# Last product of a SwiGLU layer by pairs of column blocks, part of it with seven products for eight; gate2 multiply-adds moved; SiLU as one activation

## The chip, the cores and the metric

The kernel runs on one core of a Trainium2 chip. The metric is the device time of one execution in microseconds, the median of several runs. Before the change it is 1625.05 us (three runs, 1624.05 to 1626.1).

## What is computed

One layer of a decoder trunk for 256 tokens of width 2048, in float32. The change touches its last part, the feed-forward network, and the vector gate2 that scales its result:

```python
gate, up = jnp.split(h @ w_ffn_in, 2, axis=-1)      # (256, 2048) @ (2048, 2 * 5632)
y = (jax.nn.silu(gate) * up) @ w_ffn_out            # (256, 5632) @ (5632, 2048)
x = x + gate2 * y                                   # gate2: 2048 numbers of silu(c) @ w_ada
```

Everything ahead of it (norms, three token mixers, their projections) is the same in both kernels.

## The kernel before

**Matmuls in three pieces.** Each float32 operand is kept as a rounded half `hi` and a remainder `lo`; `mm3` (L169 to L172) makes a product of three matmuls, hi x hi (L170), hi x lo (L171), lo x hi (L172). The activations stand in the array, transposed, 128 x 128 at a time; the weights move through it in 512 columns. A "chunk" is 128 of the inner dimension, a "column block" 512 output columns, and the 256 tokens are two tiles.

**Weights.** A DMA on SP's queue (`raw_tile`, L159) brings two chunks of one column block, 512 KB. The scalar engine rounds them to `whi` (L166), the vector engine subtracts to get `wlo` (L167; a "split" in the text). `whi` and `wlo` have four buffers each (`halves_room`), `raw` has four too, and in the FFN's first product two scratch tiles, A4 and A8, serve as further raw tiles. A split's buffers come free when TensorE is through with the weights four splits back. In `block` one such pair of chunks serves twelve matmuls: two chunks, two token tiles, three pieces.

**FFN, first product.** Eleven rounds `i` (L1283 on): in each a column block of gate (`pg`) and one of up (`pu`), sixteen chunks each, into four PSUM banks `acc`. In the rounds 1 to 10 the first four chunks of both blocks go through `chain`: the two token tiles and the two column blocks make a 2 x 2 product over two pairs of chunks, and it is done in Winograd's form of Strassen's scheme with seven products instead of eight. Seven splits are needed for it and four differences of weights (`right_sums`, L1220), and for the left side four sums, made once (`left_sums`). Partial results are added between banks (L1246, the copies L1261 and L1264); one bank, c21, gathers and is handed over several times, so a product into it waits for the addition before. The chain's first matmuls follow the round before without a pause; `later` (called behind the fifth product) transposes the activations of the round before (L1071) and splits them (L190, L191) into H, A, T and other slots. After the chain come `block(pg ...)` and `block(pu ...)` over twelve chunks. The gate block's PSUM goes through Sigmoid (L1292) and a multiply (L1293), the up block's through another multiply (L1305).

**gate2.** A generator in the background computes it (32 multiply-adds of 1024 columns on the vector engine, L287, then additions of the bias, L936, and a broadcast over the partitions with two matmuls for each half of a quarter, L945 to L952). `tick` moves it on: 0.4 of a step for each call. `block` calls it every two chunks, `chain` after each product. `flush` runs what is left, behind the first column block of the last product.

**Last product.** Four column blocks `n`, 44 chunks each, one after the other through `block`, two PSUM banks each; then `add_out` multiplies with gate2 (L1329), adds the residual (L1331) and stores. n = 3 runs its last chunks token tile by token tile, so that the end is short.

**What sets the order.** A scheduler orders each engine's queue at build time by priority: inside `prio()` instructions are put ahead as if they had been written some 4000 instructions earlier (weight loads, casts, splits, evictions), as far as their buffers allow. Every queue then runs strictly in that order.

## Time and profile before

| | |
|---|---|
| median of three runs | 1625.05 us |
| the profiled execution's own time | 1625.11 us |
| its span on the core | 1623.3 us |
| mean granted clock of TensorE | 0.995 |
| TensorE busy | 1597.2 us, 7293 matmuls |
| vector engine busy | 1215.9 us |
| scalar engine busy | 839.9 us |
| FFN's first product, rounds 1 to 10 | from about 936 to 1379 us |
| last product | from about 1379 us to the end |

All times in timelines are microseconds from the span's start. A row of a timeline has the start, the length, the engine, the line, the operation with output and inputs (buffer numbers left out), and in brackets how long the engine had idled before it and what ended that. A matmul's length is more than its share of the engine: matmuls are pipelined, and what one costs is the distance to the next one's start. The vector and scalar engines likewise start an instruction a little before the one ahead has ended. In a row of groups "x18 | 12.1, 684" means 18 instructions, 12.1 us busy, 684 ns each.

### The profile page before, as it was taken

To read this page: it belongs to the slowest core of one execution; us is meant where nothing else is said; L and a number is where in the kernel's file an instruction comes from. 1 tells how busy PE (TensorE), PEld (TensorE's weight loads), DVE (VectorE), ACT (ScalarE), POOL (GpSimd) and SP (SyncE) were. 2 spreads that over 40 slices of the span, in tenths; PEclk is the share of its full clock that TensorE was granted. 3 is DMA by queue.
4 is the path that set the end of the run, shared out by engine and by line. 5 is a ranking of instruction groups with operands and counts; after the bars stand their busy time and mean duration, and the time that the engine had idled before them with its cause. 6 is when DMAs were issued, how large, how long until landed. Compare 5 with 4: busy or idle time off the path is not lost.

```text
span 1623.3 us, 20048 instructions
## 1 busy us (share of the span) xinstructions
PE 1597.2 (98%) x7293; PEld 1316.6 (81%) x7293; DVE 1215.9 (75%) x1396; ACT 839.9 (52%) x1162; POOL 5.3 (0%) x14
## 2 busy tenths in 40 slices
PE   8999999999999999999999999999999999999999
PEld 7878888788777888888887888777888888888887
DVE  6889995887779787878757788988877776454454
ACT  5654458756587444444445555545555555333332
POOL 1000000000000000000000000000000000000000
PEclk9999999999999999999999999999999999999999
DMA  8999996884777888988777578777666667666663
GB/s 333 351 328 320 329 308 222 279 261 141 248 235 233 263 306 309 316 291 309 241 220 228 172 248 274 256 263 244 191 187 192 196 195 234 192 204 194 205 207 113
DMA packets 116179, 399.24 MB, mean 246 GB/s; under 512 B 13090, under 2 KB 13896, under 8 KB 116080
## 3 DMA queue, kind: packets, MB, share of 16 engines
q1 hardware_dynamic: 115856, 397.95, 74.6%
q8 instruction: 57, 0.93, 0.2%
q14 instruction: 42, 0.34, 0.1%
q0 software_dynamic: 224, 0.01, 0.0%
HBM read 393.71 MB, written 4.19 MB: 245 GB/s over the span
## 4 chain that ended last, share of the span: by engine, by line
PE 87%; DVE 5%; DMA 3%; ACT 2%; issue 2%; SPq 0%; DVEq 0%; ACTq 0%
PE acc L172 27%; PE acc L171 27%; PE acc L170 27%; DVE ada L287 2%; DVE wlo L167 1%; DMA AR<-ada_rest 1%; DMA raw<-w_ffn_in 1%; PE misc L1071 1%; ACT whi L166 1%; PE misc L786 1%; DMA A<-ada 1%; PE misc L171 0%; PE misc L170 0%; PE misc L172 0%; DMA raw<-w_in 0%
## 5 line engine op out<-in xcount | busy, mean ns | idle before, releaser
L167 DVE TENSOR_TENSOR wlo<-raw,whi 128x1024 fp32r<-128x1024 f32 (+1 forms) x486 | 577.3, 1195 | 295.7 <-ACT whi L166 294.1
L166 ACT CAST whi<-raw 128x1024 fp32r<-128x1024 f32 (+1 forms) x486 | 499.3, 1030 | 563.8 <-PE acc L172 443.1
L171 PE MATMUL acc<-wlo,H 128*128 128x512 f32 x1476 | 578.8, 392 | 2.5 <-DVE wlo L167 2.3
L172 PE MATMUL acc<-whi,H 128*128 128x512 f32 x1476 | 579.2, 393 | 1.0 <-DVE H L1157 0.6
L170 PE MATMUL acc<-whi,H 128*128 128x512 f32 x1476 | 578.2, 392 | 0.8 <-ACT H L442 0.4
L171 PEld LDWEIGHTS acc<-wlo,H 128*128 128x128 f32 x1476 | 278.4, 189 | 61.0 <-DVE wlo L167 4.4
L172 PEld LDWEIGHTS acc<-whi,H 128*128 128x128 f32 x1476 | 278.5, 189 | 59.6 <-DVE H L449 1.8
L170 PEld LDWEIGHTS acc<-whi,H 128*128 128x128 f32 x1476 | 278.5, 189 | 58.6 <-ACT H L442 1.3
L170 PE MATMUL acc<-whi,A 128*128 128x512 f32 x372 | 147.2, 396 | 4.5 <-DVE acc L1246 4.5
L171 PE MATMUL acc<-wlo,A 128*128 128x512 f32 x372 | 145.5, 391 | 0.6 <-DVE wlo L167 0.6
L166 ACT CAST whi<-A 128x1024 fp32r<-128x1024 f32 x90 | 94.5, 1054 | 89.1 <-PE acc L172 76.2
L167 DVE TENSOR_TENSOR wlo<-A,whi 128x1024 fp32r<-128x1024 f32 x90 | 109.1, 1222 | 33.5 <-ACT whi L166 32.8
L172 PE MATMUL acc<-whi,A 128*128 128x512 f32 x340 | 133.0, 391 | 0.0
L170 PEld LDWEIGHTS acc<-whi,A 128*128 128x128 f32 x372 | 70.1, 188 | 19.8 <-DVE acc L1246 6.0
L171 PEld LDWEIGHTS acc<-wlo,A 128*128 128x128 f32 x372 | 70.2, 189 | 15.2 <-DVE wlo L167 1.4
L287 DVE SCALAR_TENSOR_TENSOR ada<-AR,csil,ada 128x1024 f32<-128x1024 f32 x59 | 75.3, 1281 | 8.0 <-DMA AR<-ada_rest 7.9
L172 PEld LDWEIGHTS acc<-whi,A 128*128 128x128 f32 x340 | 64.1, 189 | 13.6
L170 PE MATMUL acc<-whi,T 128*128 128x512 f32 x120 | 46.7, 389 | 0.0
L171 PE MATMUL acc<-wlo,T 128*128 128x512 f32 x120 | 46.7, 389 | 0.0
L172 PE MATMUL acc<-whi,T 128*128 128x512 f32 x120 | 46.7, 389 | 0.0
L172 PE MATMUL acc<-whi,OS 128*128 128x512 f32 x112 | 43.6, 389 | 0.0
L486 ACT COPY A<-acc 128x512 f32<-128x512 f32 x50 | 29.0, 586 | 14.3 <-PE acc L172 13.0
(369 smaller groups left out, 1412.7 us busy)
## 6 DMA issues: line engine op xcount, KB each, us to landing
raw<-w_in SPq DMA_DIRECT2D x203, 512.0 KB, 5.0
raw<-w_ffn_in SPq DMA_DIRECT2D x122, 512.0 KB, 4.7
raw<-w_ffn_out SPq DMA_DIRECT2D x88, 512.0 KB, 4.2
AR<-ada_rest SPq DMA_DIRECT2D x79, 512.0 KB, 5.0
A<-w_ffn_in SPq DMA_DIRECT2D x54, 512.0 KB, 4.7
raw<-w_out SPq DMA_DIRECT2D x32, 512.0 KB, 4.6
KC<-ada_rest SPq DMA_DIRECT2D x30, 512.0 KB, 5.6
OS<-ada SPq DMA_DIRECT2D x16, 512.0 KB, 6.7
```

The source lines that it names most:

```text
L166: nc.scalar.copy(hi, raw)
L167: state["split"] = nc.vector.tensor_tensor(lo, raw, hi.bitcast(F32), op=ALU.subtract)
L170: nc.tensor.matmul(ps, lh, rh, start=start, stop=False, skip_group_check=seeded)
L171: nc.tensor.matmul(ps, lh, rl, start=False, stop=False, skip_group_check=seeded)
L172: state["mm"] = nc.tensor.matmul(ps, ll, rh, start=False, stop=stop, skip_group_check=seeded)
L287: nc.vector.scalar_tensor_tensor(acc, raw, c, acc, op0=ALU.mult, op1=ALU.add)
L486: nc.scalar.copy(A[b][:, t, :], pss[t])
L786: nc.tensor.matmul(ps[:n, t * N_GLA + h, :].rearrange("p (s l) -> p s l", l=L), at(f, h, t)[:, :n], odd(at(f, h, t)), start=True, stop=True,)
L1071: nc.tensor.transpose(ps[:, i, :], src[:, i * P : (i + 1) * P], ident)
```

## The change

Three things are changed. Lines named after L1200 have other numbers in the changed kernel: the differences are L1226 there, the last difference in its own place is L1242, the left side's sums L1207 to L1214, the additions between banks L1252, the multiply with the up block L1315, the load of the residual L1327, Silu L1303, and `add_out` L1339 and L1341.

1. The last product goes by pairs of column blocks (0 and 1, 2 and 3). The first eight chunks of each pair (four of its 22 chunk pairs) go through `chain` with seven products, each over two groups of chunk pairs, so each product has 12 matmuls. The left side's sums for it are made in the rounds 8 and 9, of the activations of the rounds 0 and 1, in the slots KC, AR0, AR1 and A15. The scratch tiles are A13, A14, H2 and H3, and H4 to H7 serve as further raw tiles; H0 to H7 hold the FFN's input until its first product is over.
2. `chain` no longer calls `tick`.
3. Sigmoid and multiply become one activation, Silu. The differences use two scratch tiles a group instead of three in turn.

```diff
@@ -1197,13 +1197,14 @@
     state["rate"] = RATE_FFN
     ring["tags"] = ("AR0", "AR1", "KC")
     act = []
-
-    sums = [S(tag, [P, 4, 2, P], F32R) for tag in ("A2", "A3")]
-
-    def left_sums(hi, lo):
-
-        full, raw = S("A13", [P, 4, T]), S("A14", [P, 4, 2, P])
-        nc.vector.tensor_tensor(full, h2[0][0].bitcast(F32), h2[1][0].bitcast(F32), op=ALU.add)
+    act_sums = []
+    LATE = {8: ("KC", "AR0"), 9: ("AR1", "A15")}
+
+    def left_sums(tags, scratch, xh, xl):
+
+        hi, lo = (S(tag, [P, 4, 2, P], F32R) for tag in tags)
+        full, raw = S(scratch[0], [P, 4, T]), S(scratch[1], [P, 4, 2, P])
+        nc.vector.tensor_tensor(full, xh.bitcast(F32), xl.bitcast(F32), op=ALU.add)
         (a0, a1), (b0, b1) = ([full[:, c : c + 2, t * P : (t + 1) * P] for t in range(NT)] for c in (0, 2))
         nc.vector.tensor_tensor(raw[:, 0], a1, b1, op=ALU.add)
         nc.vector.tensor_tensor(raw[:, 1], raw[:, 0], a0, op=ALU.subtract)
@@ -1211,33 +1212,38 @@
         nc.vector.tensor_tensor(raw[:, 3], b0, raw[:, 1], op=ALU.subtract)
         nc.scalar.copy(hi, raw)
         nc.vector.tensor_tensor(lo, raw, hi.bitcast(F32), op=ALU.subtract)
-
-    def right_sums(src, b0, b1):
-
-        def differ(x, y):
-            d = S(f"A{13 + state['turn'] % 3}", [P, 2, NB])
-            state["turn"] += 1
-            nc.vector.tensor_tensor(d, x, y, op=ALU.subtract)
-            return d
+        return hi, lo
+
+    def right_sums(src, b0, b1, places):
 
         def halved(raw):
             hi, lo = halves_room()
             halve(hi, lo, raw)
             return hi, lo
 
+        def differ(tag, x, y):
+            d = S(tag, [P, 2, NB])
+            nc.vector.tensor_tensor(d, x, y, op=ALU.subtract)
+            return d
+
+        out = []
         with prio():
-            b11, b12 = raw_tile(src, 0, b0), raw_tile(src, 0, b1)
-            b22, b21 = raw_tile(src, 2, b1), raw_tile(src, 2, b0)
-            out = [halved(b11)]
-            t1 = differ(b12, b11)
-            out.append(halved(t1))
-            t2 = differ(b22, t1)
-            out += [halved(t2), halved(b21)]
-            out.append(halved(differ(b22, b12)))
-            out += [halved(b22), halved(differ(b21, t2))]
+            raws = [(raw_tile(src, 4 * g, b0), raw_tile(src, 4 * g, b1)) for g in range(len(places))]
+            raws = [r + (raw_tile(src, 4 * g + 2, b0), raw_tile(src, 4 * g + 2, b1)) for g, r in enumerate(raws)]
+            out += [halved(b11) for b11, b12, b21, b22 in raws]
+            t1 = [differ(p[0], r[1], r[0]) for p, r in zip(places, raws)]
+            out += [halved(t) for t in t1]
+            t2 = [differ(p[1], r[3], t) for p, r, t in zip(places, raws, t1)]
+            out += [halved(t) for t in t2]
+            out += [halved(r[2]) for r in raws]
+            out += [halved(differ(p[0], r[3], r[1])) for p, r in zip(places, raws)]
+            out += [halved(r[3]) for r in raws]
+            for t, r in zip(t2, raws):
+                nc.vector.tensor_tensor(t, r[2], t, op=ALU.subtract)
+            out += [halved(t) for t in t2]
         return out
 
-    def chain(lefts, rights, c11, c21, c12, c22):
+    def chain(lefts, sums, rights, c11, c21, c12, c22):
 
         side, held = misc_bank([P, NB]), scr([P, NB])
 
@@ -1248,14 +1254,15 @@
         rights = iter(rights)
 
         def product(ps, left, first=False):
-            hi, lo = next(rights)
-            for i in range(2):
-                h, l = left(i)
-                mm3(ps, h, l, hi[:, i, :], lo[:, i, :], first and i == 0, i == 1, seeded=True)
-            tick(state["rate"])
-
-        total = lambda q: lambda i: (sums[0][:, q, i, :], sums[1][:, q, i, :])
-        part = lambda c, t: lambda i: lefts(c + i, t)
+            for g in range(len(sums)):
+                hi, lo = next(rights)
+                for i in range(2):
+                    h, l = left(g, i)
+                    begin, end = first and g == i == 0, g == len(sums) - 1 and i == 1
+                    mm3(ps, h, l, hi[:, i, :], lo[:, i, :], begin, end, seeded=True)
+
+        total = lambda q: lambda g, i: (sums[g][0][:, q, i, :], sums[g][1][:, q, i, :])
+        part = lambda c, t: lambda g, i: lefts(4 * g + c + i, t)
         product(c11, part(0, 0), True)
         with prio(2 * AHEAD):
             nc.scalar.copy(c21, c11)
@@ -1267,12 +1274,12 @@
         product(c11, part(2, 0))
         product(c21, total(2))
         add(c22)
-        with tc.issue_after(state["mm"].ins), prio():
-            later.pop()()
+        if later:
+            with tc.issue_after(state["mm"].ins), prio():
+                later.pop()()
         product(c12, total(3))
         product(c21, part(2, 1))
 
-    state["turn"] = 0
     for i in range(NFF):
         pg = [acc_bank() for _ in range(NT)]
         if i == 0:
@@ -1283,18 +1290,21 @@
             pu = [acc_bank() for _ in range(NT)]
         else:
             pu = [acc_bank() for _ in range(NT)]
-            chain(h2_at, right_sums(w_ff, i, NFF + i), *pg, *pu)
+            chain(h2_at, h2_sums, right_sums(w_ff, i, NFF + i, [("A13", "A14")]), *pg, *pu)
+            if i in LATE:
+                assert not macs
+                with prio():
+                    act_sums.append(left_sums(LATE[i], ("A13", "A14"), *act[i - min(LATE)]))
             block(pg, h2_at, w_ff, 4, KC, i, go_on=True, seeded=True)
         sgs = []
         with prio():
             for t in range(NT):
                 sg = scr([P, NB])
-                nc.scalar.activation(sg, pg[t], AF.Sigmoid)
-                nc.vector.tensor_mul(sg, sg, pg[t])
+                nc.scalar.activation(sg, pg[t], AF.Silu)
                 sgs.append(sg)
         if i == 0:
             block(pu, h2_at, w_ff, 0, KC, NFF)
-            left_sums(*sums)
+            h2_sums = [left_sums(("A2", "A3"), ("A13", "A14"), h2[0][0], h2[1][0])]
             rooms["extra"] = ("A4", "A8")
         else:
             block(pu, h2_at, w_ff, 4, KC, NFF + i, go_on=True, seeded=True)
@@ -1335,29 +1345,35 @@
     KF = 4 * NFF
     CUT = KF - 14
     w_fo = I["w_ffn_out"]
+    K0 = 4 * len(act_sums)
     for n in range(4):
-        pss = [acc_bank() for _ in range(NT)]
+        if n % 2 == 0:
+            rooms["extra"] = ("H4", "H5", "H6", "H7")
+            both = [[acc_bank() for _ in range(NT)] for _ in range(2)]
+            rights = right_sums(w_fo, n, n + 1, [("A13", "A14"), ("H2", "H3")])
+            chain(act_at, act_sums, rights, *both[0], *both[1])
+        pss = both[n % 2]
         if n == 3:
-
-            block(pss, act_at, w_fo, 0, CUT, n, more=True)
+            rooms["extra"] = ()
+            block(pss, act_at, w_fo, K0, CUT, n, more=True, go_on=True, seeded=True)
             w = load_weights(w_fo, CUT, KF, n, spare=[f"H{j}" for j in range(2, 8)])
-            block(pss, act_at, None, CUT, KF, 0, w=w, tiles=(0,), go_on=True)
+            block(pss, act_at, None, CUT, KF, 0, w=w, tiles=(0,), go_on=True, seeded=True)
             with prio():
                 add_out(n, 0, pss[0])
 
-            block(pss, act_at, None, CUT, KF - LASTK, 0, w=w, tiles=(1,), go_on=True, more=True)
+            block(pss, act_at, None, CUT, KF - LASTK, 0, w=w, tiles=(1,), go_on=True, more=True, seeded=True)
             side = acc_bank()
             for cols, ps in ((slice(0, NB - LASTC), pss[1][:, : NB - LASTC]), (slice(NB - LASTC, NB), side[:, :LASTC])):
                 for k in range(KF - LASTK, KF):
                     wh, wl = w[k - CUT]
                     h, l = act_at(k, 1)
-                    mm3(ps, h, l, wh[:, cols], wl[:, cols], k == KF - LASTK and cols.start > 0, k == KF - 1)
+                    mm3(ps, h, l, wh[:, cols], wl[:, cols], k == KF - LASTK and cols.start > 0, k == KF - 1, seeded=True)
                 if cols.start == 0:
                     add_out(n, 1, pss[1], end=NB - LASTC)
                     add_out(n, 1, pss[1], NB - LASTC, store=False)
             add_out(n, 1, side, NB - LASTC, base=NB - LASTC)
         else:
-            block(pss, act_at, w_fo, 0, KF, n)
+            block(pss, act_at, w_fo, K0, KF, n, go_on=True, seeded=True)
             if n == 0:
                 flush()
                 gate2 = state["gate2"]
```

How the change moves instructions, at three places. On the vector engine behind the chain of round i = 9, where TensorE goes on to `block(pg ...)` and needs its first split. Before, from behind the last split of the chain (acc is the PSUM addition, wlo a split, OS2 and OS1 the transposed activations of the round before):

```order
L1246 TENSOR_TENSOR acc_2323_10920<-acc_2322_10919,scr_2348_10967 128x512
L167 TENSOR_TENSOR wlo_2343_10957<-raw_2327_10926,whi_2342_10956 128x1024
L167 TENSOR_TENSOR wlo_2346_10963<-A15_2344_10960,whi_2345_10962 128x1024
L1246 TENSOR_TENSOR acc_2324_10921<-acc_2322_10919,scr_2348_10967 128x512
L167 TENSOR_TENSOR wlo_2353_11031<-raw_2351_11028,whi_2352_11030 128x1024
L191 TENSOR_TENSOR OS2_2320_10915<-misc_2349_11002,OS1_2319_10914 128x4x128
L191 TENSOR_TENSOR OS2_2320_10915<-misc_2350_11009,OS1_2319_10914 128x4x128
L167 TENSOR_TENSOR wlo_2356_11037<-A4_2354_11034,whi_2355_11036 128x1024
```

Now (A13 and A14 are scratch, A5 and A6 activations of round 1, A15 and AR1 the new sums):

```order
L1252 TENSOR_TENSOR acc_2307_10857<-acc_2306_10856,scr_2331_10903 128x512
L167 TENSOR_TENSOR wlo_2327_10894<-raw_2312_10865,whi_2326_10893 128x1024
L167 TENSOR_TENSOR wlo_2329_10899<-A14_2318_10877,whi_2328_10898 128x1024
L1252 TENSOR_TENSOR acc_2308_10858<-acc_2306_10856,scr_2331_10903 128x512
L1207 TENSOR_TENSOR A13_2336_10966<-A5_1788_8422,A6_1789_8423 128x1024
L191 TENSOR_TENSOR OS2_2304_10852<-misc_2332_10938,OS1_2303_10851 128x4x128
L191 TENSOR_TENSOR OS2_2304_10852<-misc_2333_10945,OS1_2303_10851 128x4x128
L1209 TENSOR_TENSOR A14_2337_10967<-A13_2336_10966 128x256
L1211 TENSOR_TENSOR A14_2337_10967<-A13_2336_10966 128x256
L1210 TENSOR_TENSOR A14_2337_10967<-A14_2337_10967,A13_2336_10966 128x256
L167 TENSOR_TENSOR wlo_2340_10978<-raw_2338_10975,whi_2339_10977 128x1024
L1212 TENSOR_TENSOR A14_2337_10967<-A13_2336_10966,A14_2337_10967 128x256
```

The next block's first split stood right behind the PSUM addition; now the first of the new sums, the two splits of the transposed activations and three additions stand ahead of it.

On the vector engine at the start of the last product. Before (scr is the product of gate and up, H1 and H0 are the activations of round 10):

```order
L167 TENSOR_TENSOR wlo_2458_11511<-raw_2456_11508,whi_2457_11510 128x1024
L167 TENSOR_TENSOR wlo_2469_11603<-raw_2467_11600,whi_2468_11602 128x1024
L167 TENSOR_TENSOR wlo_2472_11609<-raw_2470_11606,whi_2471_11608 128x1024
L167 TENSOR_TENSOR wlo_2475_11615<-raw_2473_11612,whi_2474_11614 128x1024
L1305 TENSOR_TENSOR scr_2439_11472<-scr_2439_11472,acc_2393_11256 128x512
L1305 TENSOR_TENSOR scr_2440_11475<-scr_2440_11475,acc_2394_11257 128x512
L167 TENSOR_TENSOR wlo_2478_11621<-raw_2476_11618,whi_2477_11620 128x1024
L167 TENSOR_TENSOR wlo_2481_11627<-raw_2479_11624,whi_2480_11626 128x1024
L167 TENSOR_TENSOR wlo_2484_11633<-raw_2482_11630,whi_2483_11632 128x1024
```

Now (H5 and H7 hold the first column block of the first and the second group, H6 and raw_2464 the second, H2, H3, A13 and A14 differences):

```order
L946 TENSOR_TENSOR T6_2450_11498<-ada_1706_7984,T6_2450_11498 128x256
L167 TENSOR_TENSOR wlo_2470_11582<-H5_2461_11565,whi_2469_11581 128x1024
L1226 TENSOR_TENSOR A13_2473_11589<-H6_2462_11567,H5_2461_11565 128x1024
L1226 TENSOR_TENSOR A14_2479_11601<-raw_2466_11575,A13_2473_11589 128x1024
L1315 TENSOR_TENSOR scr_2430_11432<-scr_2430_11432,acc_2383_11210 128x512
L1315 TENSOR_TENSOR scr_2431_11434<-scr_2431_11434,acc_2384_11211 128x512
L1226 TENSOR_TENSOR H2_2474_11591<-raw_2464_11571,H7_2463_11569 128x1024
L167 TENSOR_TENSOR wlo_2472_11586<-H7_2463_11569,whi_2471_11585 128x1024
L167 TENSOR_TENSOR wlo_2476_11594<-A13_2473_11589,whi_2475_11593 128x1024
L167 TENSOR_TENSOR wlo_2478_11598<-H2_2474_11591,whi_2477_11597 128x1024
L1226 TENSOR_TENSOR H3_2480_11603<-H4_2468_11579,H2_2474_11591 128x1024
L167 TENSOR_TENSOR wlo_2482_11606<-A14_2479_11601,whi_2481_11605 128x1024
```

Where one split followed another there are differences between them, and the one that reads H7 stands ahead of the splits that follow.

On SP's queue at the same place. Before:

```order
L159 DMA raw_2467_11600<-w_ffn_out 128x1024
L159 DMA raw_2470_11606<-w_ffn_out 128x1024
L159 DMA raw_2473_11612<-w_ffn_out 128x1024
L1317 DMA A4_2463_11594<-x2_far_6951 128x1024
L1317 DMA A8_2464_11596<-x2_far_6951 128x1024
L159 DMA raw_2476_11618<-w_ffn_out 128x1024
L159 DMA raw_2479_11624<-w_ffn_out 128x1024
L159 DMA raw_2482_11630<-w_ffn_out 128x1024
L159 DMA raw_2485_11636<-w_ffn_out 128x1024
```

Now:

```order
L1327 DMA A8_2456_11559<-x2_far_6951 128x1024
L159 DMA H5_2461_11565<-w_ffn_out 128x1024
L159 DMA raw_2467_11577<-w_ffn_out 128x1024
L159 DMA H6_2462_11567<-w_ffn_out 128x1024
L159 DMA H5_2507_11755<-w_ffn_out 128x1024
L159 DMA H7_2463_11569<-w_ffn_out 128x1024
L159 DMA H7_2513_11767<-w_ffn_out 128x1024
L159 DMA H6_2510_11761<-w_ffn_out 128x1024
```

The loads went into the raw tiles alone; now four of the first eight go to H4 to H7, and a load to H5 for a later block stands ahead of that to H7.

## Prediction

> **What bounds the kernel now.** I read the page first, then a timeline of TensorE in a chain of seven products, then the vector engine there, then TensorE's waits. On the page:
>
> ```profile
> span 1623.3 us, 20048 instructions
> PE 1597.2 (98%) x7293; PEld 1316.6 (81%) x7293; DVE 1215.9 (75%) x1396; ACT 839.9 (52%) x1162; POOL 5.3 (0%) x14
> DVE  6889995887779787878757788988877776454454
> ```
>
> TensorE works 98% of the span, so a matmul less is time less, and a wait of TensorE is time more. The vector engine has room on average, most of it in the last product (the fours and fives), but an average says nothing of a short stretch. What a matmul costs is its distance to the next (PE, start, length):
>
> ```profile
> 1337.10 0.39 PE L170 MATMUL misc<-whi,A 128*128 128x512 f32 x1
> ...
> 1338.46 0.39 PE L170 MATMUL acc<-whi,A 128*128 128x512 f32 x1
> ...
> 1342.54 1.03 PE L1071 MATMUL misc<-ident,scr 128*128 128x128 f32 x8
> 1343.33 0.48 PE L170 MATMUL acc<-whi,A 128*128 128x512 f32 x1
> ```
>
> Six matmuls, one chunk pair of one product (a "part" from here on), take 1.36 us, 0.227 us each; eight transposes take 0.79. The vector engine in the same chain:
>
> ```profile
> 1324.25 1.22 DVE L1220 TENSOR_TENSOR A<-A,A 128x1024 f32<-128x1024 f32 x1
> 1325.38 1.22 DVE L167 TENSOR_TENSOR wlo<-raw,whi 128x1024 fp32r<-128x1024 f32 x1
> 1326.52 1.22 DVE L1220 TENSOR_TENSOR A<-A,A 128x1024 f32<-128x1024 f32 x1
> ...
> 1335.45 1.28 DVE L1305 TENSOR_TENSOR scr<-scr,acc 128x512 f32<-128x512 f32 x2
> ...
> 1340.08 0.70 DVE L1246 TENSOR_TENSOR acc<-acc,scr 128x512 f32<-128x512 f32 x1
> 1340.68 2.35 DVE L167 TENSOR_TENSOR wlo<-A,whi 128x1024 fp32r<-128x1024 f32 x2
> ...
> 1344.68 1.28 DVE L191 TENSOR_TENSOR KD<-misc,OD 128x512 fp32r<-128x512 f32 x2
> ```
>
> A split (L167) or a difference (L1220) takes 1.13 us, 512 columns out of PSUM 0.60. Seven parts need seven splits and four differences: 11 x 1.13 / 7 = 1.78 us of vector work for 1.36 us of TensorE. **A chain is fed from a lead**, and the lead is four pairs of buffers, since whi and wlo have four each. In an ordinary block one split serves twelve matmuls (2.73 us). The chains do run dry today: these are the longest of TensorE's waits (total, times, longest).
>
> ```profile
> PE acc L170 <- DVE acc L1246: 4.5, 3, 1.5
> PE acc L171 <- DVE wlo L167: 2.9, 4, 1.0
> ```
>
> The copy that follows each chain's first product shows the length of the rounds (ACT, start):
>
> ```profile
> 980.48 0.57 ACT L1261 COPY acc<-acc 128x512 f32<-128x512 f32 x1 [0.26 <-PE acc L172]
> 1023.71 0.57 ACT L1261 COPY acc<-acc 128x512 f32<-128x512 f32 x1 [0.26 <-PE acc L172]
> 1071.20 0.57 ACT L1261 COPY acc<-acc 128x512 f32<-128x512 f32 x1 [0.26 <-PE acc L172]
> 1116.13 0.57 ACT L1261 COPY acc<-acc 128x512 f32<-128x512 f32 x1 [0.26 <-PE acc L172]
> 1162.84 0.57 ACT L1261 COPY acc<-acc 128x512 f32<-128x512 f32 x1 [0.30 <-PE acc L172]
> ```
>
> The second round takes 43.23 us, the next three 47.49, 44.93 and 46.71: 9.4 us lost. One of them, on TensorE and on the vector engine:
>
> ```profile
> 1030.49 0.80 PE L170 MATMUL acc<-whi,A 128*128 128x512 f32 x1 [1.52 <-DVE acc L1246]
> 1031.09 0.63 PE L171 MATMUL acc<-wlo,A 128*128 128x512 f32 x1
> 1031.51 0.63 PE L172 MATMUL acc<-whi,A 128*128 128x512 f32 x1
> ```
>
> ```profile
> 1027.41 1.22 DVE L167 TENSOR_TENSOR wlo<-A,whi 128x1024 fp32r<-128x1024 f32 x1
> 1028.55 1.28 DVE L287 SCALAR_TENSOR_TENSOR ada<-AR,csil,ada 128x1024 f32<-128x1024 f32 x1
> 1029.75 0.69 DVE L1246 TENSOR_TENSOR acc<-acc,scr 128x512 f32<-128x512 f32 x1
> ```
>
> A gate2 multiply-add (L287) stands ahead of the PSUM addition for which TensorE waits; and after the wait the matmuls follow at 0.43 us instead of 0.227, so the wait costs more than itself.
>
> **The change part by part**, against this execution (1625.11 us, 1.8 outside its span, next to the median of 1625.05).
>
> *Matmuls.* Two groups of chunks in two pairs of column blocks, four in all, go from eight parts to seven: 4 x 6 = 24 matmuls fewer (7293 to 7269), 24 x 0.227 = **-5.5**. Nothing hides TensorE, so this is sure.
>
> *No multiply-adds inside FFN chains.* **-9.4**, the whole loss of the three rounds, is the upper bound; zero is the lower. I take it all, and book what comes in its place: differences now have two scratch tiles, not three, so the third and fourth can't be made ahead. In the chains of i = 2 and 6 the order puts the last difference behind the sixth split. From the chain's start: evictions to 1.4, splits to 4.8, addition 5.4, split 6.5, difference 7.7, its cast 1.05, last split done at 9.9. TensorE wants it at 6 x 1.36 + 0.79 + 0.2 = 9.2: 0.7 late; then two L191 (1.2) and the next block's first split (1.13) come 0.9 late. 2 x 1.6, and 0.1 in each of six others: **+3.8** (0 to 6). The multiply-adds, now spread over more rounds, fit between splits of blocks.
>
> *Sums of the left side* (i = 8, 9). They have a priority, and the order puts their first addition (1.13), two L191 (1.2) and three additions of 256 columns ahead of the next block's first split:
>
> ```profile
> L1208 DVE TENSOR_TENSOR A<-A x1: 422/422/422, 914.3 to 914.3; 128x256 f32<-128x256 f32 x1
> L1210 DVE TENSOR_TENSOR A<-A x1: 422/422/422, 914.6 to 914.6; 128x256 f32<-128x256 f32 x1
> ```
>
> 0.33 each. From the PSUM addition's end at 8.3: 9.4, 10.6, 11.6, split done 12.7; TensorE is through its seven parts and transposes at 10.4 and wants it at 10.6. 2 x 2.1 = **+4.2** (0 to 6).
>
> *SiLU.* Removes 20 multiplies in these rounds (two more before them):
>
> ```profile
> L1293 DVE TENSOR_TENSOR scr<-scr,acc 128x512 f32<-128x512 f32 x18 | 12.1, 684 | 2.5 <-ACT scr L1292 2.5
> ```
>
> Nobody on TensorE waits for them: the second block of the round covers them. Silu itself is not in the trace; I take Sigmoid's price, and the number of table loads stays the same. Zero (-1 to +1).
>
> *First chain of the last product* (n = 0, 14 parts). The right side of the second part lies in H7, and H7 is read by the last matmuls of the FFN's first stage. So its load starts only when they end, behind a load to H5 that SP issues first. What a load takes:
>
> ```profile
> DMA to landing us min/median/max: 3.6/3.9/4.2
> ...
> raw<-w_ffn_in SPq DMA_DIRECT2D x122, 512.0 KB, 4.7
> ...
> L166 ACT CAST whi<-raw 128x1024 fp32r<-128x1024 f32 x169 | 178.2, 1054 | 230.6 <-PE acc L172 222.1 <-DMA raw<-w_ffn_in 4.4 <-issue 3.7
> ```
>
> (Loads of w_ffn_out in the steady stretch, loads of the stage before, and the cast.) Landed at 3.9 to 6.2 after the block's end; I take 5.0, since two go at once. Cast 1.05: TensorE, dry from 1.4, goes on at 6.1. In the vector queue all that is left of the chain stands behind the difference that reads H7: by the order 19 operations of 1.13 and two additions of 0.60, 22.7 us, so the last split ends at 27.8. With its last matmuls and small hand-overs the chain ends at 29.4; 14 x 1.36 + 0.79 = 19.9 would do. Two L191 then delay the next block's first split by 0.6. **+10** (7 to 12).
>
> *Broadcast of gate2.* Before, it was over in the FFN; now flush leaves its last piece in n = 1's first tiles, where its second matmul stands behind the four operations of add_out (2.4) and a split: **+0.6** (0 to 1.5).
>
> *Chain of n = 2.* Here the lead exists: loads run ahead, and the first three splits and four differences are made in the block before, which has room:
>
> ```profile
> 1443.00:1503.00 60.00, 60.00 (x266) 49.70 (x265) 29.26 (x26) 23.37 (x23) 0.00 (x0) 1.00 0.68 202
> ```
>
> (PE 60.00 of 60, DVE 29.26.) From the block's end: four operations of add_out 2.4, 11 splits and four differences 17.0, two additions 1.2, so 20.8, and with the last part 22.3 against 19.1: **+3.2** (0 to 6).
>
> *Clock.* If waits make matmuls slow as at 1030.49, the chain of n = 0 loses little (the vector engine bounds it), that of n = 2 up to 2: **+1** (0 to 4). The same wait of 1.5 us at 1123.51 left the next matmuls at 0.23, so the row alone doesn't decide:
>
> ```profile
> 1123.51 0.50 PE L170 MATMUL acc<-whi,A 128*128 128x512 f32 x1 [1.51 <-DVE acc L1246]
> 1123.85 0.39 PE L171 MATMUL acc<-wlo,A 128*128 128x512 f32 x1
> 1124.08 0.40 PE L172 MATMUL acc<-whi,A 128*128 128x512 f32 x1
> ```
>
> [...]
>
> Sum: -5.5 - 9.4 + 3.8 + 4.2 + 10 + 0.6 + 3.2 + 1 = +7.9, which gives **1633.0 us**.
>
> **The rivals.** About 0.2%, 3.3 us, is what a measurement of this kernel can tell from no change. *Faster:* the vector engine comes into the chains with more lead than I walked, since it has 22 multiplies less and no multiply-add inside. If it is 2.1 us earlier in the rounds i = 2, 6, 8 and 9 and at n = 2, the terms for which it is late stand at their lower ends, 0.6 for the six rounds, zero, zero for n = 2 and the clock, and 7 in the first chain if H7 too lands at its earliest: 1625.1 - 5.5 - 9.4 + 0.6 + 7 + 0.6 = 1618.4. For it speaks that the 9.4 us go whenever the multiply-adds do; against it the order, in which the late operations stand between two that TensorE waits for, whatever came before. *No change:* half of the eight in FFN rounds and of the four after n = 0 come, and the first chain costs 9: 1633.0 - 4 - 2 - 1 = 1626. *Slower still:* the slow matmuls hold through both 14-part chains. A part then takes 2.6 us, more than the vector work of 1.78; over half of each chain, 7 x 1.2 in n = 2 and some in n = 0 give 1633 + 9 = 1642. For it speaks that both chains idle again and again; against it 1123.51. That the matmuls don't fall by 24 is excluded by the order (6749 rows to 6725).
>
> **How the numbers follow.** Forecast 0.63, faster 0.10, no change 0.12, slower still 0.15. The forecast's own bounds (the first chain 8.5 to 12, the other terms partly together) reach 1627 to 1639; about 0.04 of its chance lies under 1628.3 and counts as no change. So faster 0.10, same 0.16, slower 0.74. Leaving out the faster case and half of the slowest, the range is 1622 to 1642.
>
> **What would show it.** Right: TensorE idle for some 4.7 us at the start of the last product, ended by a cast that a load to H7 released; then waits for L167 all through that chain; rounds of 43 us at i = 3 to 5, and 45 at i = 8 and 9. PE's count 7269. Wrong: chains of 14 parts that take 19 to 20 us, or rounds still over 44 us at i = 3 to 5.

## The result and the profile after

The changed kernel takes 1636.95 us (median of four runs, 1635.72 to 1637.97); the kernel before took 1624.55 us beside it. The ratio is 1.0078, with a 95% interval of 1.0061 to 1.0095: **slower by 0.8%**. The forecast was 1633.0 us, in a range of 1622 to 1642. The profiled execution took 1637.97 us with a span of 1636.2; before, the span was 1623.3. So there are 12.9 us to place.

The page of the changed kernel:

```profile
span 1636.2 us, 20051 instructions
PE 1598.8 (98%) x7269; PEld 1313.2 (80%) x7269; DVE 1240.3 (76%) x1418; ACT 854.5 (52%) x1180; POOL 5.3 (0%) x14
DVE  6889996878779787878757778888888775755754
```

TensorE has the 24 matmuls less, and yet is not busy for less time: a matmul that runs slowly is recorded with 0.63 us instead of 0.39, and the first one behind a wait with 0.50. The fives and fours of the vector engine at the end have become fives and sevens, but for the last slices.

For the places in time, three starts on TensorE are enough: the first matmul of the last product (n = 0), the first of n = 2, the last matmul of all. Before (PE, start, length):

```profile
1378.81 0.39 PE L170 MATMUL acc<-whi,A 128*128 128x512 f32 x1
...
1499.40 0.39 PE L170 MATMUL acc<-whi,A 128*128 128x512 f32 x1
...
1619.12 0.28 PE L172 MATMUL acc<-H,H 128*128 128x256 f32 x1
```

After:

```profile
1378.84 0.39 PE L170 MATMUL acc<-whi,A 128*128 128x512 f32 x1
...
1509.83 0.39 PE L170 MATMUL acc<-whi,A 128*128 128x512 f32 x1
...
1631.98 0.28 PE L172 MATMUL acc<-H,H 128*128 128x256 f32 x1
```

The last product begins at the same time in both (+0.03). Its first pair of column blocks takes 130.99 us for 120.59, its second 122.15 for 119.72. So the whole loss, 10.4 + 2.4, lies in the last product, and the FFN, which lost its three long waits and got others, comes out even.

**Inside the FFN.** The copy after each chain's first product marks the rounds (ACT; i = 1 to 6, 8 and 10 are shown). After:

```profile
938.07 0.57 ACT L1268 COPY acc<-acc 128x512 f32<-128x512 f32 x1 [0.30 <-PE acc L172]
981.13 0.57 ACT L1268 COPY acc<-acc 128x512 f32<-128x512 f32 x1 [0.26 <-PE acc L172]
1025.55 0.57 ACT L1268 COPY acc<-acc 128x512 f32<-128x512 f32 x1 [0.30 <-PE acc L172]
1068.60 0.57 ACT L1268 COPY acc<-acc 128x512 f32<-128x512 f32 x1 [0.30 <-PE acc L172]
1112.86 0.57 ACT L1268 COPY acc<-acc 128x512 f32<-128x512 f32 x1 [0.31 <-PE acc L172]
1156.60 0.57 ACT L1268 COPY acc<-acc 128x512 f32<-128x512 f32 x1 [0.26 <-PE acc L172]
...
1246.00 0.57 ACT L1268 COPY acc<-acc 128x512 f32<-128x512 f32 x1 [0.30 <-PE acc L172]
...
1336.80 0.57 ACT L1268 COPY acc<-acc 128x512 f32<-128x512 f32 x1 [0.30 <-PE acc L172]
```

Before, the group of the same ten copies, with its first and last start, and the broadcast's matmuls (L950; each has one of L951 behind it):

```profile
L1261 ACT COPY acc<-acc x10: 570/570/570, 937.4 to 1337.3; 128x512 f32<-128x512 f32 x10
L950 PE MATMUL misc<-T,ones_r x8: 281/281/281, 1177.1 to 1276.1; 128*128 128x256 f32 x8
```

Round 1 takes 43.06 us in both kernels; nine such would be 387.5. Before, the nine took 399.9, after 398.7. Of the 12.4 us that the rounds before had above that, the eight pairs of broadcast matmuls are 1.9 (a pair takes 0.24 us), the waits of the chains 10.4. After, rounds 2 to 7 have 264.87 - 6 x 43.06 = 6.5 us above it, rounds 8 and 9 90.80 - 86.12 = 4.7. Rounds 3 to 5, which lost most before, take 43.05, 44.26 and 43.74. The broadcast has moved:

```profile
L950 PE MATMUL misc<-T,ones_r x8: 281/281/374, 1324.1 to 1461.8; 128*128 128x256 f32 x8
```

One pair is left in these rounds, two stand in round 10, five in the first half of the last product (1.2 us there).

**What a wait costs.** Three rows of round 2 and the two longest waits of rounds 8 and 9, of a matmul that waits for a split (PE of after):

```profile
988.65 0.40 PE L170 MATMUL acc<-whi,H 128*128 128x512 f32 x1
989.34 0.50 PE L171 MATMUL acc<-wlo,H 128*128 128x512 f32 x1 [0.29 <-DVE wlo L167]
989.68 0.39 PE L172 MATMUL acc<-whi,H 128*128 128x512 f32 x1
...
1257.91 0.50 PE L171 MATMUL acc<-wlo,H 128*128 128x512 f32 x1 [1.61 <-DVE wlo L167]
...
1302.66 0.50 PE L171 MATMUL acc<-wlo,H 128*128 128x512 f32 x1 [1.39 <-DVE wlo L167]
```

The wait is listed with 0.29, but the two steps around it are 0.69 and 0.34 where 0.227 each is usual: 0.57 is lost. A matmul is recorded here with 0.39, 0.16 more than the 0.227 to the next start, and the first one after a wait with 0.50, 0.11 longer. Each wait costs some 0.28 more than the number in brackets (0.27 to 0.29 at each of the eleven waits of the rounds 2 to 9). Rounds 2 to 7 have eight waits of 3.6 us in all, with 8 x 0.28 some 5.9 of the 6.5.

**The left sums**, in the vector queue of round 8 (DVE of after), from the chain's last addition to the split that TensorE waits for:

```profile
1252.71 0.69 DVE L1252 TENSOR_TENSOR acc<-acc,scr 128x512 f32<-128x512 f32 x1
1253.31 1.21 DVE L1207 TENSOR_TENSOR A<-A,A 128x1024 f32<-128x1024 f32 x1
1254.44 1.28 DVE L191 TENSOR_TENSOR OS<-misc,T 128x512 fp32r<-128x512 f32 x2
1255.64 0.41 DVE L1209 TENSOR_TENSOR A<-A 128x256 f32<-128x256 f32 x1
...
1256.64 1.21 DVE L167 TENSOR_TENSOR wlo<-A,whi 128x1024 fp32r<-128x1024 f32 x1
```

**The first chain of the last product** on TensorE, and the vector queue behind H7:

```profile
1386.01 0.79 PE L170 MATMUL acc<-whi,A 128*128 128x512 f32 x1 [5.64 <-ACT whi L166]
...
1387.55 0.63 PE L171 MATMUL acc<-wlo,A 128*128 128x512 f32 x1
1387.97 0.63 PE L172 MATMUL acc<-whi,A 128*128 128x512 f32 x1
...
1403.11 0.50 PE L171 MATMUL acc<-wlo,AR 128*128 128x512 f32 x1 [0.81 <-DVE wlo L167]
...
1410.47 0.61 PE L170 MATMUL acc<-whi,A 128*128 128x512 f32 x2
```

```profile
1384.84 1.22 DVE L1226 TENSOR_TENSOR H<-raw,H 128x1024 f32<-128x1024 f32 x1 [2.59 <-DMA H<-w_ffn_out]
1385.99 1.23 DVE L167 TENSOR_TENSOR wlo<-H,whi 128x1024 fp32r<-128x1024 f32 x1
...
1406.97 1.22 DVE L167 TENSOR_TENSOR wlo<-H,whi 128x1024 fp32r<-128x1024 f32 x1
```

TensorE has done one part, then idles 5.64 us until the load to H7 is there and cast. From 1384.84 to 1408.19 the vector engine works almost without a gap. TensorE, slow until 1392.6, has caught up with it at 1400 and then waits three times, last at 1403.11. The row at 1410.47 is the first of the block behind the chain: 31.6 us for what needs 19.9.

**The chain of n = 2** (PE of after):

```profile
1523.98 0.50 PE L170 MATMUL acc<-whi,AR 128*128 128x512 f32 x1 [0.84 <-ACT whi L166]
1524.93 0.50 PE L170 MATMUL acc<-whi,KC 128*128 128x512 f32 x1 [0.45 <-ACT whi L166]
1526.24 0.80 PE L171 MATMUL acc<-wlo,AR 128*128 128x512 f32 x1 [0.80 <-DVE wlo L167]
1526.83 0.63 PE L172 MATMUL acc<-whi,A 128*128 128x512 f32 x1
1527.25 0.63 PE L170 MATMUL acc<-whi,AR 128*128 128x512 f32 x1
```

Three waits in a row, then matmuls 0.43 us apart instead of 0.227.

### The profile page after: what moved, and what is told of

It reads as the page before. It is cut to its first block, busy times and chain, and to the rows that moved or that the text cites. A ratio compares the mean times of both kernels' runs of the same rounds, so it can differ in the third digit from the quotient of the medians.

```text
span 1636.2 us, 20051 instructions
## 1 busy us (share of the span) xinstructions
PE 1598.8 (98%) x7269; PEld 1313.2 (80%) x7269; DVE 1240.3 (76%) x1418; ACT 854.5 (52%) x1180; POOL 5.3 (0%) x14
## 4 chain that ended last, share of the span: by engine, by line
PE 87%; DVE 6%; DMA 3%; ACT 2%; issue 1%; POOL 0%; DVEq 0%; ACTq 0%; POOLq 0%
PE acc L172 26%; PE acc L171 26%; PE acc L170 26%; DVE wlo L167 3%; DMA AR<-ada_rest 1%; ACT whi L166 1%; PE acc L430 1%; PE misc L786 1%; PE misc L170 1%; PE misc L171 1%; PE misc L1071 1%; PE misc L172 1%; DVE ada L287 1%; DMA raw<-w_in 0%; PE misc L423 0%
## 5 line engine op out<-in xcount | busy, mean ns | idle before, releaser
L166 ACT CAST whi<-raw 128x1024 fp32r<-128x1024 f32 (+1 forms) x449 | 459.9, 1027 | 486.8 <-PE acc L172 376.7
L167 DVE TENSOR_TENSOR wlo<-raw,whi 128x1024 fp32r<-128x1024 f32 (+1 forms) x449 | 531.4, 1191 | 233.0 <-ACT whi L166 231.2
L166 ACT CAST whi<-A 128x1024 fp32r<-128x1024 f32 x98 | 103.0, 1054 | 94.8 <-PE acc L172 86.5
L170 PE MATMUL acc<-whi,A 128*128 128x512 f32 x332 | 131.4, 397 | 7.6 <-ACT whi L166 5.6
L167 DVE TENSOR_TENSOR wlo<-A,whi 128x1024 fp32r<-128x1024 f32 x98 | 118.7, 1218 | 24.1 <-ACT whi L166 24.1
L171 PE MATMUL acc<-wlo,A 128*128 128x512 f32 x332 | 129.9, 391 | 0.0
L172 PE MATMUL acc<-whi,A 128*128 128x512 f32 x312 | 122.6, 393 | 0.0
L170 PEld LDWEIGHTS acc<-whi,A 128*128 128x128 f32 x332 | 62.6, 189 | 22.3 <-ACT whi L166 6.1
L166 ACT CAST whi<-H 128x1024 fp32r<-128x1024 f32 x41 | 43.0, 1053 | 64.0 <-PE acc L172 39.4
L167 DVE TENSOR_TENSOR wlo<-H,whi 128x1024 fp32r<-128x1024 f32 x41 | 49.8, 1221 | 35.0 <-ACT whi L166 34.9
L171 PEld LDWEIGHTS acc<-wlo,A 128*128 128x128 f32 x332 | 62.6, 189 | 12.6 <-DVE wlo L167 0.4
L172 PEld LDWEIGHTS acc<-whi,A 128*128 128x128 f32 x312 | 59.2, 190 | 12.4
```

The lines of the kernel that those rows point to most:

```text
L166: nc.scalar.copy(hi, raw)
L167: state["split"] = nc.vector.tensor_tensor(lo, raw, hi.bitcast(F32), op=ALU.subtract)
L170: nc.tensor.matmul(ps, lh, rh, start=start, stop=False, skip_group_check=seeded)
L171: nc.tensor.matmul(ps, lh, rl, start=False, stop=False, skip_group_check=seeded)
L172: state["mm"] = nc.tensor.matmul(ps, ll, rh, start=False, stop=stop, skip_group_check=seeded)
```

## Experiments

The theory: the change trades the waits for multiply-adds against as many new ones in the FFN (two scratch tiles, left sums), and loses in the two chains of 14 parts, where the vector engine has 1.78 us of work for each 1.36 of TensorE and, at n = 0, begins late because H7 does. Rivals stand with each run. Each ratio is to the kernel before, run beside it on the same chip. On the chips of the experiments the kernel before has medians of 1623.24, 1622.28 and 1623.56 us, so ratios are compared, not times. A single execution is a weak witness for the whole: in the eleven traces the first copy of the FFN's chains starts between 933.6 and 939.9 us, though the kernels hardly differ ahead of it. So traces are compared stage by stage.

**Without the multiply-adds, nothing else.** One line of the kernel before goes, in `product` of `chain`:

```diff
-            tick(state["rate"])
```

> The kernel before, with the one line taken out by which a chain moves the gate2 work on; nothing else. Theory (the multiply-adds inside the chains make TensorE wait, and elsewhere they have room): the rounds 3 to 5 fall from 47.5, 44.9 and 46.7 to 43.1 to 43.5 us, so -9, and the broadcast's last step behind the first column block gives 0.6 back: 1615.5 to 1617. Rival (the vector engine is short of time over the whole FFN, so the waits only move to later rounds): 1621 to 1625, with rounds 6 to 9 longer by what 3 to 5 lose.

1615.25 us (1614.93 to 1618.7), ratio 0.9956 [0.9939, 0.9973]. Its copies:

```profile
L1260 ACT COPY acc<-acc x10: 570/570/570, 937.2 to 1325.4; 128x512 f32<-128x512 f32 x10
```

388.2 us for nine rounds, 43.1 each: the chains lose nothing any more, and no wait of TensorE is listed in them. Of the 11.7 us that the rounds win, 1.3 are broadcast that moves: the first pair of column blocks takes 121.9 us for 120.6. By the medians the kernel gains 8.0 us, by the two traces 10.0; the forecast had 9.4 for the change's gain in the FFN. This one line beats both kernels.

**The changed FFN with the last product as before.**

```diff
-            if i in LATE:
+            if False:
...
+    PLAIN = (0, 1, 2, 3)
...
```

There are no left sums, and the column blocks in `PLAIN` go through plain blocks.

> The changed kernel's FFN (no gate2 steps in chains, two scratch tiles for the differences, Silu) with the last product as before, in plain blocks, and without the left sums in the rounds 8 and 9. Theory (two scratch tiles put differences late and cost what the trace after shows in rounds 2, 4, 6): 3 to 4 us more than the run with the line alone taken out, 1619 to 1621. Rival (the waits in those rounds are from the gate2 steps, now in the blocks, and scratch tiles cost nothing): the same as that run within 1 us, 1616 to 1617.

1621.87 us, ratio 0.9991 [0.9979, 1.0003].

```profile
L1268 ACT COPY acc<-acc x10: 570/570/570, 939.2 to 1334.3; 128x512 f32<-128x512 f32 x10
```

395.1 us, 6.9 more than the run before: of the 11.7 us that the one edit wins in these rounds, 6.9 are given back inside the FFN. The rival (same as the one edit) falls; the theory had the loss 1 to 3 us too small. What remained open is which part of the changed FFN does it.

**SiLU in one step, three scratch tiles.** The run without the multiply-adds, with one more edit:

```diff
-                nc.scalar.activation(sg, pg[t], AF.Sigmoid)
-                nc.vector.tensor_mul(sg, sg, pg[t])
+                nc.scalar.activation(sg, pg[t], AF.Silu)
```

> The kernel before, without the multiply-adds that each product of a chain released, and with SiLU as one step; three scratch tiles for the differences. Theory (SiLU costs nothing, and the 6.6 us by which the changed FFN alone was slower than the one edit come from the two scratch tiles and the order that goes with them): 1615 to 1616.5 us, rounds of 43.1 us throughout. Rival (SiLU as one step is what made rounds 2, 4, 6 and 7 longer): 1619 to 1622 us.

1617.13 us, ratio 0.9967 [0.9955, 0.9978], which overlaps that of the one edit.

```profile
L1260 ACT COPY acc<-acc x10: 570/570/570, 936.7 to 1324.9; 128x512 f32<-128x512 f32 x10
```

A little above the range expected, but 388.2 us again in the rounds. SiLU costs and gains nothing there; the 6.9 us belong to the two scratch tiles and the order of operations written for them, the only other difference that these rounds have (the two were not taken apart).

**Left sums without their priority.**

```diff
-                with prio():
-                    act_sums.append(left_sums(LATE[i], ("A13", "A14"), *act[i - min(LATE)]))
+                act_sums.append(left_sums(LATE[i], ("A13", "A14"), *act[i - min(LATE)]))
```

> The changed kernel, with the left sums of rounds 8 and 9 without their priority. Theory (they delay the first split of the next block by 1.6 and 1.4 us, and each wait costs some 0.3 more than it lists): rounds 8 and 9 fall from 45.8 and 45.0 to about 43.5, and the kernel to 1632 to 1634 us. Rival (the rounds are late for another cause, the two scratch tiles as in round 7): 1636 to 1638 us.

1633.05 us, ratio 1.0069 [1.0049, 1.0089]. Its interval overlaps that of the changed kernel; beside it on the same chip the kernel with twenty more matmuls (below), which is as slow as the changed one, took 1637.48. The rounds say it more sharply:

```profile
L1268 ACT COPY acc<-acc x10: 570/570/570, 937.9 to 1333.4; 128x512 f32<-128x512 f32 x10
```

395.5 us for 398.7. 3.2 of the 4.4 us were the priority.

**Only the second pair of column blocks by the chain.**

```diff
+    PLAIN = (0, 1)
...
```

> The changed kernel with column blocks 0 and 1 in plain blocks, 12 matmuls more, and only 2 and 3 by the chain; left sums kept. Theory (the first chain's wait for H7 and the vector work behind it is the main loss, 11 to 12 us against 2.7 saved): 1626 to 1629. Rival (both chains lose alike, being short of vector work alike): half of some 16 us of waits, 1631 to 1633.

1626.46 us, ratio 1.0023 [1.001, 1.0035], some 9 us below the changed kernel by the ratios. In the trace the first pair takes 121.9 us for 131.0, with 12 matmuls more: the first chain is what makes the difference. In the chain of n = 2:

```profile
1518.11 0.50 PE L170 MATMUL acc<-whi,KC 128*128 128x512 f32 x1 [0.45 <-ACT whi L166]
1519.42 0.50 PE L171 MATMUL acc<-wlo,AR 128*128 128x512 f32 x1 [0.81 <-DVE wlo L167]
1519.75 0.39 PE L172 MATMUL acc<-whi,A 128*128 128x512 f32 x1
```

The waits of the changed kernel return within 0.02, but the matmuls behind them are 0.23 to 0.33 apart, not 0.43.

**H7 not needed early.** The turn of the raw tiles starts over at the second of the four ordinary ones, so that H7 is the seventh tile loaded for the first chain, not the third:

```diff
             rooms["extra"] = ("H4", "H5", "H6", "H7")
+            rooms["n"] = 1
```

> The changed kernel with one line more, which starts the round of raw tiles elsewhere: the first column blocks of both groups now lie in raw tiles, and H7 holds the one that the eighth part needs. The same work, count for count. Theory (in the first chain TensorE and the vector queue stand until H7 has landed, and then the vector engine has 22.7 us of work): the vector engine starts at the block's end, ends about 6 us earlier, and the first chain loses about 4 instead of 11.6: 1629 to 1630.5. Rival (the chain is bound by its vector work alone, wherever the data lie, or by the slow clock): 1634 to 1637.

1629.53 us, ratio 1.0031 [1.0018, 1.0044]: some 7.6 us less by the ratios. The long wait is gone; the chain still has short ones, the longest late in it:

```profile
1391.57 0.49 PE L170 MATMUL acc<-whi,AR 128*128 128x512 f32 x1 [0.85 <-ACT whi L166]
```

In this trace the first chain takes 27.1 us for 31.6, so only 4.6 less. But it is the slowest of this kernel's executions, and behind the last wait, from 1393.2 to 1399.9, TensorE's granted clock is 0.50: from that wait to the next block it takes 10.3 us, in the changed kernel 7.4. Without this the late load makes some 7.5 of the first chain's 11.7 us; the rest is like what the chain of n = 2 loses.

**TensorE kept at work during the wait for H7.** Twenty matmuls into an unused bank behind the chain's first part:

```diff
+                if first and g == 0 and state.pop("fill", 0):
+                    spare = misc_bank([P, NB])
+                    for _ in range(20):
+                        with tc.issue_after(state["mm"].ins), prio(2 * AHEAD):
+                            nc.tensor.matmul(spare, ones_r, hi[:, 0, :], start=True, stop=True)
...
```

(`fill` is set at n = 0.)

> The changed kernel, with 20 matmuls into an unused bank between the first and the second part of the first chain of the last product, so that TensorE works (4.5 us) while it waits for H7. Theory (the vector queue bounds that chain from the moment H7 is there, so what TensorE does meanwhile doesn't matter): 1636 to 1638 us, and the slow matmuls (0.43 us apart) behind the wait are gone or cost nothing. Rival (the idle time lowers TensorE's clock and the eleven slow matmuls, some 2.3 us, are part of the loss): 1633 to 1635 us.

1637.48 us, ratio 1.0099 [1.008, 1.0119].

```profile
1379.46 4.83 PE L1267 MATMUL misc<-whi,ones_r 128*128 128x512 f32 x20
1385.64 0.50 PE L170 MATMUL acc<-whi,A 128*128 128x512 f32 x1 [1.36 <-ACT whi L166]
...
1402.26 0.51 PE L171 MATMUL acc<-wlo,AR 128*128 128x512 f32 x1 [0.80 <-DVE wlo L167]
```

The wait shrinks to 1.36 us and the slow matmuls behind it are gone, but the later waits are there and nothing is gained. The last of them ends 24.2 us behind the chain's start (1378.10) here and 24.3 in the changed kernel, though H7 landed 0.4 later here: up to there the slow matmuls cost half a microsecond at most, since the vector engine sets the pace. The total alone wouldn't show it, because slow matmuls come here too, only later: the granted clock is 0.50 from 1403.12 to 1406.53, where no wait covers it, and from the last wait to the next block TensorE takes 9.0 us for 7.4.

**Fewer differences in the long chains.** The second group's raw tiles are split instead of its differences, so part of the product is left out:

```diff
+            one = lambda p, x, y: differ(p, x, y) if p[0] == "A" else x
-            t1 = [differ(p[0], r[1], r[0]) for p, r in zip(places, raws)]
+            t1 = [one(p[0], r[1], r[0]) for p, r in zip(places, raws)]
...
```

> The changed kernel without the four differences of the second group in each of the two chains of 14 parts (n = 0 and n = 2): that group's raw tiles are split instead, so its sums on the right side are left out of the computation. Theory (both chains are bound by the vector engine's work in one queue, 1.13 us for a difference): the waits for splits in the chain of n = 2 go, about 4 us, and the chain of n = 0 falls by about 3 to 4.5, so 1628 to 1630 us. Rival (the four pairs of buffers that splits go into, and the hand-over from TensorE that frees them, bound the chains): at most 2 us less in all, 1635 to 1637.

1632.38 us, ratio 1.0053 [1.0039, 1.0067], about 4 us less than the changed kernel by the ratios: between the two expectations, so neither stands as put.

```profile
1385.81 0.79 PE L170 MATMUL acc<-whi,A 128*128 128x512 f32 x1 [5.52 <-ACT whi L166]
...
1525.81 0.50 PE L171 MATMUL acc<-wlo,A 128*128 128x512 f32 x1 [0.77 <-DVE wlo L167]
```

At n = 2 it went as the theory has it: of the waits two are left, and the extra time of the second pair falls from 5.2 to 2.1 us (1.0 or more of that because the clock did not fall there in this execution). At n = 0 it falls only from 11.7 to 9.3. With the vector queue lighter, the idle time before H7 and the slow matmuls behind it, which the vector queue had covered, are on the path themselves. The theory had forgotten that a second bound stands close under the first.

**A candidate.** One group by seven products in each pair of column blocks (12 matmuls less than before), three scratch tiles everywhere, one set of left sums without priority, no load to H4 to H7 ahead of the last product:

```diff
-    LATE = {8: ("KC", "AR0"), 9: ("AR1", "A15")}
+    LATE = {8: ("KC", "AR0")}
...
-            chain(h2_at, h2_sums, right_sums(w_ff, i, NFF + i, [("A13", "A14")]), *pg, *pu)
+            chain(h2_at, h2_sums, right_sums(w_ff, i, NFF + i, [("A13", "A14", "A15")]), *pg, *pu)
...
-            rooms["extra"] = ("H4", "H5", "H6", "H7")
-            rights = right_sums(w_fo, n, n + 1, [("A13", "A14"), ("H2", "H3")])
+            rights = right_sums(w_fo, n, n + 1, [("A13", "A14", "A15")])
```

> A candidate: the changed kernel with one group of chunks by seven products in each pair of column blocks (12 matmuls fewer than before, not 24), three scratch tiles for the differences everywhere, one set of left sums without priority, and no load to H4 to H7 before the last product. Theory (with three scratch tiles a chain of seven parts loses nothing, and the last product's chains then gain 12 x 0.227 = 2.7 us): 1612 to 1614.5 us, below the 1615.25 of the one edit alone. Rival (the chains of the last product lose by themselves, whatever the scratch tiles, because four splits are all the lead there is): 1615 to 1618 us.

1613.75 us, ratio 0.9951 [0.9932, 0.997]: faster than both kernels. Its waits for splits, all of the program:

```profile
PE acc L171 <- DVE wlo L167: 1.4, 2, 1.0
```

On the same chip it is 3.4 us below the run with SiLU and no multiply-adds; 12 matmuls are worth 2.7. The traces place only a part of that: the last product takes 239.8 us for 241.6, but the rounds take 390.6 for 388.2, since TensorE waits for additions in the rounds 5 and 6, and why these come late there was not looked into. Against the one edit alone the intervals overlap, so whether it is the faster of the two is not settled.

## Why the prediction was right

The direction and the mechanisms were right; the time came out 4 us above the forecast, from terms that were sized too small. Of its signs, TensorE's idle time at the start of the last product, ended by the cast of H7, came with 5.64 us for 4.7, the rounds 8 and 9 with 45.8 and 45.0. Two came otherwise. The waits behind it do not run all through the first chain: from 1387 to 1400 TensorE has none, being slow at first, and only then three. And round 4 takes 44.26 us, over the 44 that the prediction had named as a sign of being wrong; its two waits, 0.27 for a split and 0.32 for an addition, are of the scratch tiles' part. By the terms of the sum, in us, forecast and then the trace of after against that of before:

| term | forecast | measured |
|---|---|---|
| 24 matmuls fewer | -5.5 | -5.5 (7293 to 7269) |
| no multiply-adds in FFN chains | -9.4 | -10.4 |
| two scratch tiles | +3.8 | +6.5 |
| left sums, rounds 8 and 9 | +4.2 | +4.4 |
| SiLU | 0 | 0 |
| first chain of the last product | +10 | +11.7 |
| broadcast of gate2 | +0.6 | -1.7 in the FFN, +1.7 behind it |
| chain of n = 2, and the clock | +3.2 + 1 | +5.2 |
| ahead of the FFN's first copy (varies by up to 6 between traces) | - | +0.7 |
| sum | +7.9 | +12.6 of 12.9 |

**Multiply-adds.** That they were the whole loss of the rounds is shown by the run without them. The forecast took three rounds; the others had another us.

**Two scratch tiles: the step that was off most.** The lateness was walked for i = 2 and 6, twice 1.6; the waits do come there, and with 0.28 more for each cost 2.8. But TensorE waits also in rounds 4, 5 and 7, mostly for the addition L1252, which costs 3.0, where 0.1 each was booked. That the listed time of all eight, 3.6, is near the term is chance. The run with the changed FFN alone and that with SiLU and three tiles show that it is this part, the tiles and the order written for them together.

**Left sums.** 2.1 was expected for each; the walk gave their place in the queue, the addition, two L191, three small additions, then the split, and the rows are in that order. The waits were 1.6 and 1.4, with what follows them 4.4. The run without the priority confirms the cause, for 3.2 of it.

**First chain.** The forecast had TensorE go on at 6.1 us from the chain's start and the last split end at 27.8. It went on at 1386.01 - 1378.84 = 7.2 and the last split ended at 1408.19 - 1378.84 = 29.4. H7 landed some 6 after the block's end (1384.81; its load took 4.5), not 5.0, inside the author's bounds of 3.9 to 6.2, and the vector work behind it took 23.4 for 22.7. That the vector queue, not TensorE's clock, bounds it is shown by the run with twenty matmuls, whose last wait ends at the same place; that H7 is the larger part, by the run that needs it late.

**Broadcast.** The forecast put a wait in n = 1. There is none; instead seven of the eight pairs of matmuls moved, 1.7 us out of the FFN's rounds and as much into round 10 and the last product. That cost nothing in the sum, but read stage by stage the FFN looks that much better than it is.

**Chain of n = 2.** The waits listed are 0.84 + 0.45 + 0.80 = 2.1, with 0.28 each 2.9, for 3.2; the five slow matmuls another 1.0, as the clock's term had it, and this is luck: in three other traces the same three waits bring no slow matmuls. The rest is steps of 0.1 to 0.2 that are not listed as waits. The run with fewer differences shows the vector work as the cause here. (The terms of this walk, 2.4, 17.0 and 1.2, make 20.6 and not 20.8.)

**Rivals.** The faster case fell: none of the late terms in the rounds 2, 6, 8 and 9 or at n = 2 stood at its lower end. No change fell with the first chain, which alone is worth more than the margin. Slower still, with slow matmuls through both chains, was wrong: they last some 12 matmuls behind the long wait, where nobody waits for them, and five at n = 2.

## What to carry to other kernels

Here fewer matmuls paid only while another engine's lead lasted: a chain of seven parts is fed from four buffered splits and the work of the block ahead, one of 14 parts isn't, and the last product of the short version with 12 matmuls saved took 239.8 us for 241.6 where that of the long one with 24 took 253.1 for 240.3. Where a change bundles edits, cost each and try the cheapest alone: here one deleted line gave 8 us, and the rest of the bundle took back more than twice as much. And before a buffer is reused for an early load, look for its last reader: here a load of 4.5 us that had to stay behind the stage's last matmuls, with the cast of 1.04 after it, made TensorE wait 5.64 us.

## What the runs showed of the hardware

At the eleven waits of the rounds 2 to 9 a wait of TensorE costs more than the profile lists, 0.28 us each (0.57 for a listed 0.29): those of 0.3 us lose about twice what they add up to.

The three waits of n = 2 agree within 0.02 in two kernels, 0.84, 0.45 and 0.80 in the changed one, 0.86, 0.45 and 0.81 with the second pair alone; in the first matmuls followed at 0.43 us, in the second at the usual pace. So the waits alone don't decide it. What differs is the granted clock, here by stretches (length; PE busy, with the number of matmuls; granted clock; DMA share and GB/s), two of the changed kernel and one with the second pair alone:

```profile
1522.26:1525.67 3.41, 1.88 (x6) 1.00 0.52 141
1525.67:1529.08 3.41, 2.84 (x7) 0.50 0.97 329
...
1517.35:1520.77 3.42, 2.17 (x8) 1.00 0.85 285
```

In the traces of both kernels each fall of the clock to 0.50 lies on a grid of 3.413 us (the falls at 1382.31 and 1525.67 are 42 steps apart), wherever the waits lie on it, and, but for the last one at the span's end, lasts one to three steps, 3.41 to 10.24 us. In the step ahead of the fall at 1525.67 five matmuls begin (the sixth of the row began earlier), 1.1 us of work at 0.227 each; ahead of the fall at 1382.31, and of that at 1030.18 in the kernel before, it is also five. With the second pair alone the waits lie otherwise on the grid: seven begin in that step, 1.6 us, and the clock stays. In these four steps, then, the clock fell after matmuls for a third of the step (1.1 us, three times) and stayed after nearly half (1.6 us, once). The fall at 1525.67 came without a long idle: no wait at n = 2 is listed with more than 0.84 us. The long idle of 5.64 us was followed by slow matmuls in every run that had it (5.52 and 6.16 us in two others), and not where twenty matmuls filled it.
